# One token block's group norm moved into the recurrence's last four steps, and the output weights into memory that frees earlier

## The chip, the cores and the metric

One core of a Trainium2 chip runs the whole kernel. The metric is the device time of one execution in microseconds (us).

## What is computed

One layer of a backbone over 2048 latent tokens of width 1024, with 256 context tokens, all in float32. The parts that matter here, cut from the reference:

```
    h = modulate(rmsnorm(x, norm1_g), shift1, scale1)
...
    q, k, v, rw, gl = jnp.split(h @ w_in, IN_SPLITS, axis=-1)
...
    ya = latent_window_attention(q, k, v, kc, vc, sink)
...
    for d, rev in enumerate((False, True)):
...
        _, y_d = wkv7_scan(S_ctx, r_l, dec_l, kk_l, b_l, k_l, v_l, rev, True)
...
    yr = rwkv_output(y_lat[0] + y_lat[1], r_l, v_l, hg_l, dirs_l, gate_g2, r_k, lnx_w, lnx_b)
    x = x + gate1 * merge_branches(ya, yr, gl, w_branch_attn, w_branch_rwkv, w_out)
    x = x + gate2 * sq_relu_mlp(modulate(rmsnorm(x, norm2_g), shift2, scale2), w_mlp_up, w_mlp_down)

def rwkv_output(y, r, v, hg, dirs, gate_g2, r_k, lnx_w, lnx_b):
...
    mu = jnp.mean(y, axis=-1, keepdims=True)
    var = jnp.mean(jnp.square(y - mu), axis=-1, keepdims=True)
    yn = (y - mu) * lax.rsqrt(var + LNX_EPS)
...
    out = (yn.reshape(B, L, RWKV_WIDTH) * lnx_w + lnx_b + bonus.reshape(B, L, RWKV_WIDTH)).astype(hg.dtype)
    g = jax.nn.sigmoid(hg) @ gate_g2
    return out * g

def merge_branches(ya, yr, gate_logits, w_branch_attn, w_branch_rwkv, w_out):
    ga, gr = jnp.split(jax.nn.sigmoid(gate_logits), N_BRANCHES, axis=-1)
    return (ga * (ya @ w_branch_attn) + gr * (yr @ w_branch_rwkv)) @ w_out
```

Each float32 matmul runs as three: every operand is split in a high part (rounded by ScalarE) and a low part (the rest, by GpSimd or VectorE), and hi x hi, lo x hi and hi x lo are added up in PSUM.

## The kernel before

The program has four stages. The first makes projections and the recurrence's inputs. The second is the recurrence in 36 steps of 64 tokens per direction (`chain_g`, `chain_u`, `chain_s`, tiles `ch`, `gb`, `tb`), grouped in nine windows of four; while a window runs, the small triangular inverses of the next are made in the tiles `ga`, `st`, `au` and `itmp` of the pool `ip`, so that in the last window these lie idle. Tokens 512 to 1023 have their last contribution from either direction long before the last window. Each step has six parts; after each part `beside` adds a piece of the attention (`attend`, 16 blocks and a tail), and a piece of the filler (`fill`: gates, then `branch` for four blocks t = 0..3 of 512 tokens, the product of the attention's output with `w_branch_attn`, eight column tiles j of 12 matmuls each, tile `gt`, L988 to L990; VectorE scales each by its gate at L991 and the result is stored to `ma_d`). Block t = 3 can only begin when the last attention block is stored (`ya_d`). At the head of each step one piece of `ada2` is made as well (tile `adp`: four of the six modulation vectors, from 32 loads of 512 KB).

The third stage (merge, L1108 to L1263) goes over four blocks of 512 tokens in the order 1, 0, 2, 3. For a block, `rwkv_out` (L1139) does group norm, affine and gate, token tile by token tile, then splits the result in `yr_h` and `yr_l`. A loop over eight column tiles j multiplies by `w_branch_rwkv` (tile `mb`, L1240 to L1242, 96 matmuls a block), and VectorE adds the attention's part and the gate (tile `gt`, two buffers, L1243 and L1244) before the split to `m_h` and `m_l`. Then 192 matmuls a block multiply by `w_out` (tile `mm`, L1258 to L1260), and `second_norm` prepares the channel mixer's input in `h2_d`. In block 1 alone `merge_weights` (L1202) stands behind the j loop: it spreads gate1 and gate2 over the partitions (`dg` L1212), then for each of eight k loads 512 KB of `w_out` into the two-buffer tile `x1t` (L1220), multiplies it by gate1 on VectorE (L1223, two halves), and splits it in `wo_h` (ScalarE, L1224) and `wo_l` (GpSimd and VectorE by turns, L1225). The fourth stage is the channel mixer (L1265 to the end; up-projection tile `fu`, down-projection tile `fd`), whose first loads (`split_raw`, L1283) share two `raw` buffers.

The order on each engine is fixed before the run: a scheduler goes through the program with a time simulation, and what it decides stands in each engine's queue. SyncE (SP) alone issues all DMAs, in its own queue's order, so that a load that waits for a buffer holds up every DMA behind it. Pools are laid out in SBUF in the order in which they are opened; a tile that lies over memory of an earlier pool waits for the last user of that memory.

Of the kernel before, what the change touches and what calls it, by code (L numbers as in the profile page):

```python
# [7 lines left out]
F32 = mybir.dt.float32  # L8
# [8 lines left out]
P = 128  # L17
D = 1024
# [29 lines left out]
def tile_hybrid_block(ctx: ExitStack, tc: tile.TileContext, io: dict, out: bass.AP):  # L48
# [14 lines left out]
    ya_d = dram.tile([NP, P, SEQ], F32, name="ya_d")  # L63
    ma_d = dram.tile([KC, P, SEQ], F32, name="ma_d")
    bon_d = dram.tile([NP, P, SEQ], F32, name="bon_d")
    sg_d = dram.tile([96, SEQ], F32, name="sg_d")
# [487 lines left out]
    def bank(pl, name, tag):  # L554
        return pl.tile([P, 512], F32, name=name, tag=tag)
# [463 lines left out]
    def fill():  # L1019
# [17 lines left out]
        for t in range(SEQ // GBL):  # L1037
            while outs < (t + 1) * GBL // P:
                yield
            yield from branch(brp, raw_of, wa, t)  # L1040

    att, flr = attend(), fill()
    TICKS, EARLY = 1.0, 24
    credit = 0.0

    def beside(ticks):
# [6 lines left out]
        if credit >= 1:  # L1053
            next(att, None)
            credit -= 1

    mods = (x for m in range(4) for x in ada2(m))
    sts = []
# [16 lines left out]
    for w in range(NWIN):  # L1075
        ahead_of = window(w + 1, sts) if w + 1 < NWIN else iter(())
        for step in range(w * WS, w * WS + WS):
            nxts = [open_step(step + 1, d) if step + 1 < NCH else None for d in range(2)]
            for part in range(6):
                if part == 0:  # L1080
                    for s in cur:
                        chain_g(s)
                    next(mods, None)
                elif part == 1:
                    for s in cur:
                        chain_u(sts[w], s)
                elif part == 2:
                    chain_s(cur, nxts)
                elif part == 3 and nxts[0] is not None:
                    for s in nxts:  # L1090
                        turn(s)
                elif part > 3 and nxts[0] is not None:
                    before(nxts[part - 4])
                next(ahead_of, None)
                beside(TICKS)
            cur = nxts
        for _ in ahead_of:
            pass
    for _ in att:
        pass  # L1100
    for _ in flr:
        pass
    p2.close()
# [9 lines left out]
    gate2 = late.tile([P, D], F32, name="gate2")  # L1113
    p3 = ExitStack()
    mo = p3.enter_context(tc.tile_pool(name="mo", bufs=1, reuse_waits="tile"))
    mw = p3.enter_context(tc.tile_pool(name="mw", bufs=1, reuse_waits="tile"))
    mb = p3.enter_context(tc.tile_pool(name="mb", bufs=2, reuse_waits="tile"))
    mp = p3.enter_context(tc.tile_pool(name="mp", bufs=2, reuse_waits="tile"))
    mpb = p3.enter_context(tc.tile_pool(name="mpb", bufs=3, space=PSUM, reuse_waits="tile"))
# [19 lines left out]
    def rwkv_out(tb):  # L1139

        t0 = tb * TB
        yT = mp.tile([P, NP, TB], F32, name="yT", bufs=1)
        for i in range(TB // C):
# [54 lines left out]

    wo_h = mo.tile([P, KC, D], F32R, name="wo_h")
    wo_l = mo.tile([P, KC, D], F32R, name="wo_l")  # L1200

    def merge_weights():  # L1202
# [3 lines left out]
        gate1 = [mw.tile([P, 512], F32, name="gate1", tag="wt", bufs=2) for hf in range(2)]  # L1206
        for m, half, dst in ((0, 0.5, gate1), (3, 1.0, (gate2[:, 0:512], gate2[:, 512:D]))):
            for hf in range(2):
                ps = mtr.tile([P, 512], F32, name="mt")
                for k in range(4):  # L1210
                    dg = mw.tile([P, P], F32, name="dg", tag="x1t", bufs=2)
                    dve.tensor_scalar(out=dg, in0=ident, scalar1=mod2[:, m, hf * 4 + k:hf * 4 + k + 1],  # L1212
                                      scalar2=half, op0=ALU.mult, op1=ALU.mult)
                    pe.matmul(ps[:, k * P:(k + 1) * P], ones, dg, start=True, stop=True)
                dve.tensor_copy(dst[hf], ps)

        w_out = io["w_out"].rearrange("(k p) n -> p k n", p=P)
        for k in range(KC):
            raw = mw.tile([P, D], F32, name="x1t", bufs=2)
            sp.dma_start(out=raw, in_=w_out[:, k])  # L1220
            for hf in range(2):
                cs = slice(hf * 512, (hf + 1) * 512)
                dve.tensor_tensor(out=raw[:, cs], in0=raw[:, cs], in1=gate1[hf], op=ALU.mult)  # L1223
            act.activation(wo_h[:, k], raw, AF.Copy)  # L1224
            (pool, dve)[k % 2].tensor_tensor(out=wo_l[:, k], in0=raw, in1=wo_h[:, k].bitcast(F32), op=ALU.subtract)  # L1225

    blocks = (1, 0, 2, 3)
    br = rwkv_out(blocks[0])
    for at, tb in enumerate(blocks):
        t0 = tb * TB  # L1230
        mh = mo.tile([P, KC, TB], F32R, name="m_h", bufs=1)
        ml = mo.tile([P, KC, TB], F32R, name="m_l", bufs=1)
        for j in range(KC):
# [11 lines left out]
            split(mh[:, j], ml[:, j], gt[:, 0])  # L1245
        if at == 0:
            merge_weights()
        if at + 1 < len(blocks):
            br = rwkv_out(blocks[at + 1])
        for i in range(TB // P):  # L1250
            x = mw.tile([P, D], F32, name="x1t", bufs=2)
            sp.dma_start(out=x, in_=io["x"][t0 + i * P:t0 + (i + 1) * P])
            for hf in range(2):
                cs = slice(hf * 512, (hf + 1) * 512)
                ps = mps.tile([P, 512], F32, name="mm")
                for k in range(KC):
                    lh, ll = mh[:, k, i * P:(i + 1) * P], ml[:, k, i * P:(i + 1) * P]
                    pe.matmul(ps, lh, wo_h[:, k, cs], start=(k == 0), stop=False)  # L1258
                    pe.matmul(ps, lh, wo_l[:, k, cs], start=False, stop=False)  # L1259
                    pe.matmul(ps, ll, wo_h[:, k, cs], start=False, stop=(k == KC - 1))  # L1260
                dve.tensor_tensor(out=x[:, cs], in0=ps, in1=x[:, cs], op=ALU.add)
# [227 lines left out]
```

## Time and profile before

| | us |
|---|---|
| median of 3 runs | 4223.32 |
| lowest, highest | 4220.43, 4228.75 |
| the profiled execution | 4228.56 |
| its span in the trace | 4226.8 |
| PE busy | 3865.3 (91%) |
| DVE busy | 2171.9 (51%) |
| ACT busy | 1359.5 (32%) |
| POOL busy | 1349.6 (32%) |
| mean granted clock of TensorE | 0.932 |

PE is TensorE (PEld its weight loads), DVE VectorE, ACT ScalarE, POOL GpSimd, SP SyncE (SPq, PEq: what their sequencers do). A share of busy time is a mean over stages; what a stage is worth is read from that stretch of the trace. Times within the span are given from its start.

### The profile page before, as it was taken

Reading aid. Unit: us, or ns where it says so; the run is one execution under the profiler, and the core shown is the slowest. Engines: PE = TensorE matmul, PEld = TensorE weight load, DVE = VectorE, ACT = ScalarE, POOL = GpSimd, SP = SyncE. Lnnn points to the kernel's source line nnn. Section 1 sums busy time; section 2 is a strip of 40 time slices with the busy share of each in tenths; the row PEclk is TensorE's granted clock in tenths of the full one; section 3 lists DMA queues with packets and bytes.
Section 4 is the critical chain, followed back from the end, with each engine's and each line's share of the span. In section 5 each row is a group of like instructions: output and inputs, shape, how many; then the busy total and the mean of one; then the engine's idle time right before and its main releaser. Section 6 shows DMA issues by size and latency. Waiting matters only on the chain.

```text
span 4226.8 us, 67796 instructions
## 1 busy us (share of the span) xinstructions
PE 3865.3 (91%) x26788; PEld 3148.4 (74%) x26788; DVE 2171.9 (51%) x3794; ACT 1359.5 (32%) x2476; POOL 1349.6 (32%) x1104
## 2 busy tenths in 40 slices
PE   7989978897899989888898779989999999999999
PEld 5778868785677767766676658768888888888887
DVE  3355277767576366556566364444443345444334
ACT  2353444554343333322322233331212213112121
POOL 3353555554221110000000174533433334443231
PEclk8999979897999989797897889999999999999999
DMA  6665566666544445343442545542211214211111
GB/s 236 202 195 158 161 183 188 188 185 184 164 138 138 125 131 148 106 132 96 131 139 83 158 150 179 176 154 65 70 50 40 60 41 130 69 60 60 40 55 45
DMA packets 617587, 529.95 MB, mean 125 GB/s; under 512 B 156212, under 2 KB 536340, under 8 KB 616244
## 3 DMA queue, kind: packets, MB, share of 16 engines
q1 hardware_dynamic: 617268, 525.60, 41.6%
q8 instruction: 211, 3.46, 0.3%
q14 instruction: 108, 0.88, 0.1%
HBM read 381.09 MB, written 144.38 MB: 124 GB/s over the span
## 4 chain that ended last, share of the span: by engine, by line
PE 58%; DVE 6%; DMA 4%; issue 2%; POOL 2%; SPq 1%; ACT 1%; POOLq 0%; DVEq 0%; ACTq 0%
PE fd L1343 5%; PE fd L1344 5%; PE fd L1345 5%; PE fu L235 5%; PE fu L236 5%; PE fu L237 5%; PE ch L535 5%; PE gt L947 3%; PE ops L883 3%; PE gb L535 2%; DVE au L582 1%; PE sc L835 1%; PE mm L1260 1%; PE mm L1258 1%; PE mm L1259 1%
## 5 line engine op out<-in xcount | busy, mean ns | idle before, releaser
L235 PE MATMUL acc<-hh,w_hi 128*128 128x384 f32 (+6 forms) x1304 | 457.4, 353 | 41.6 <-ACT hh L211 18.9
L237 PE MATMUL acc<-hh,w_lo 128*128 128x384 f32 (+6 forms) x1304 | 455.8, 351 | 10.3 <-POOL w_lo L229 10.3
L236 PE MATMUL acc<-hl,w_hi 128*128 128x384 f32 (+6 forms) x1304 | 456.5, 351 | 4.8 <-POOL hl L212 4.8
L1349 DVE TENSOR_TENSOR acc<-fd,acc 128x512 f32<-128x512 f32 x480 | 322.3, 686 | 249.1 <-PE fd L1345 246.8
L235 PE MATMUL fu<-h2h,up_h 128*128 128x512 f32 x1024 | 403.4, 394 | 5.8 <-ACT rl L1330 5.8
L1343 PE MATMUL fd<-dn_h,g_h 128*128 128x512 f32 x1024 | 399.8, 390 | 3.5 <-DVE acc L1347 3.5
L236 PE MATMUL fu<-h2l,up_h 128*128 128x512 f32 x1024 | 402.6, 393 | 0.0
L237 PE MATMUL fu<-h2h,up_l 128*128 128x512 f32 x1024 | 402.0, 393 | 0.0
L1333 DVE TENSOR_TENSOR g_l<-rl,g_h 128x512 fp32r<-128x512 f32 x128 | 150.0, 1173 | 487.4 <-POOL rl L1332 487.4
L1344 PE MATMUL fd<-dn_l,g_h 128*128 128x512 f32 x1024 | 399.7, 390 | 0.0
L1345 PE MATMUL fd<-dn_h,g_l 128*128 128x512 f32 x1024 | 398.3, 390 | 0.0
L235 PEld LDWEIGHTS acc<-hh,w_hi 128*128 128x128 f32 (+2 forms) x1304 | 256.1, 197 | 67.1 <-ACT hh L211 21.8
L1332 POOL TENSOR_TENSOR rl<-rl 128x512 f32<-128x512 f32 x128 | 149.9, 1171 | 469.2 <-ACT g_h L1331 469.1
L229 POOL TENSOR_TENSOR w_lo<-w_raw,w_hi 128x1024 fp32r<-128x1024 f32 (+1 forms) x92 | 232.7, 2532 | 205.9 <-ACT w_hi L228 185.7
L1330 ACT ACTIVATE rl<-fu 128x512 f32<-128x512 f32 x128 | 76.2, 597 | 654.1 <-PE fu L237 644.9
L237 PEld LDWEIGHTS acc<-hh,w_lo 128*128 128x128 f32 (+2 forms) x1304 | 255.7, 196 | 31.4 <-POOL w_lo L229 12.5
L236 PEld LDWEIGHTS acc<-hl,w_hi 128*128 128x128 f32 (+2 forms) x1304 | 256.0, 196 | 25.1 <-POOL hl L212 6.0
L1287 POOL TENSOR_TENSOR dn_l<-raw,dn_h 128x1024 fp32r<-128x1024 f32 x64 | 155.6, 2450 | 275.1 <-ACT dn_h L1286 275.1
L845 DVE TENSOR_REDUCE mm<-sc 128x1 f32<-128x256 f32 (+1 forms) x256 | 119.0, 477 | 237.9 <-PE sc L837 152.2
L235 PEld LDWEIGHTS fu<-h2h,up_h 128*128 128x128 f32 x1024 | 193.1, 189 | 49.3 <-ACT rl L1330 6.0
L1343 PEld LDWEIGHTS fd<-dn_h,g_h 128*128 128x128 f32 x1024 | 192.9, 188 | 44.9 <-DVE acc L1347 4.0
L237 PEld LDWEIGHTS fu<-h2h,up_l 128*128 128x128 f32 x1024 | 192.7, 188 | 43.5
(305 smaller groups left out, 8292.3 us busy)
## 6 DMA issues: line engine op xcount, KB each, us to landing
w_raw<-in_w_in SPq DMA_DIRECT2D x74, 512.0 KB
raw<-in_w_mlp_up SPq DMA_DIRECT2D x64, 512.0 KB
raw<-in_w_mlp_down SPq DMA_DIRECT2D x64, 512.0 KB
bk_d<-bk SPq DMA_DIRECT2D x36, 512.0 KB
w<-v_d SPq DMA_DIRECT2D x144, 128.0 KB
gw_raw<-in_w_in SPq DMA_DIRECT2D x32, 512.0 KB
ada_w<-in_w_ada SPq DMA_DIRECT2D x32, 512.0 KB
gt<-g_d SPq DMA_DIRECT2D x64, 256.0 KB
```

Of the source, the lines that this page charges most:

```text
L229: pool.tensor_tensor(out=lo[:, :, :m], in0=raw[:, :, :m], in1=hi[:, :, :m].bitcast(F32), op=ALU.subtract)
L235: pe.matmul(ps[:m, :n], wh[:, k, :m], hh[:, k, :], start=(k == 0), stop=False)
L236: pe.matmul(ps[:m, :n], wh[:, k, :m], hl[:, k, :], start=False, stop=False)
L237: pe.matmul(ps[:m, :n], wl[:, k, :m], hh[:, k, :], start=False, stop=(k == KC - 1))
L535: return self.link(nc.tensor.matmul(*a, **k))
L1287: eng.tensor_tensor(out=lo, in0=raw, in1=hi.bitcast(F32), op=ALU.subtract)
L1332: pool.tensor_tensor(out=rl, in0=rl, in1=rl, op=ALU.mult)
L1333: dve.tensor_tensor(out=glo[:, j], in0=rl, in1=gh[:, j].bitcast(F32), op=ALU.subtract)
L1343: pe.matmul(ps, lh, dn[j][0][:, cs], start=(j == 0), stop=False)
L1344: pe.matmul(ps, lh, dn[j][1][:, cs], start=False, stop=False)
L1345: pe.matmul(ps, ll, dn[j][0][:, cs], start=False, stop=(j == FG - 1))
L1349: dve.tensor_tensor(out=acc[:, cs], in0=ps, in1=acc[:, cs], op=ALU.add)
```

## The change

A new generator `early` does the group norm, affine, bonus and gate of block 1 (tokens 512 to 1023) in the last window, steps 32 to 35, in four pieces of 128 tokens, nine calls a step; it works in the inverse's idle tiles and in PSUM that the attention uses, and stores its result to `yw_d`. `rwkv_out` of block 1 is left with four loads and the split. The pieces of `ada2` come at one and two a step by turns, so that they end with step 23 and not with step 35. `merge_weights` is emitted ahead of block 1's j loop, and the spreading of gate2 behind its loop over k. The tiles `wo_h` and `wo_l` are cut into one per k; k = 0..3 lie in a new pool `mv` and k = 4..7 in `mo`, and the pool `mp` comes first, which moves every pool behind it in SBUF: `mv` now lies at the memory that the attention had, k = 4..7 over the attention branch's weights, and the channel mixer's pool `fw` (its first `up_h`, `up_l` and half of `h2`) comes to lie over `mv`. The core of the diff:

```diff
+    EB0, EBN = 512, 512
+    yw_d = dram.tile([NP, P, EBN], F32, name="yw_d")
...
+    def early():
+        wk = [ip.tile([P, 4, NP, P], F32, name="yw0", tag="ga", bufs=1), ip.tile([P, 4, NP, P], F32, name="yw1", tag="st")]
+        aw = ip.tile([P, 1024], F32, name="g2e", tag="au", bufs=1)
+        sg = ip.tile([P, 2, P], F32, name="sge", tag="itmp", bufs=1)
+        g2 = aw[0:96, 0:512]
+        sp.dma_start(out=g2, in_=io["gate_g2"])
...
+        for i in range(EBN // P):
+            yT, yc, yw, bt = (wk[i % 2][:, j] for j in range(4))
...
+            ps = bank(atp, "ey", "at")
+            for p in range(NP):
+                pe.transpose(ps[:, p * P:(p + 1) * P], yT[:, p], ident)
+            y3 = ps.rearrange("p (h c) -> p h c", c=C)
+            dve.tensor_reduce(out=s1[:, 0], in_=y3, axis=AX.X, op=ALU.add)
+            dve.tensor_scalar(out=s1[:, 0], in0=s1[:, 0], scalar1=-1.0 / C, scalar2=None, op0=ALU.mult)
...
+            dve.tensor_tensor(out=y3c, in0=y3, in1=s1[:, 0].unsqueeze(2).broadcast_to([P, H, C]), op=ALU.add)
+            act.activation(yw, yc, AF.Square)
+            dve.tensor_reduce(out=s1[:, 1], in_=yw.rearrange("p a b -> p (a b)").rearrange("p (h c) -> p h c", c=C),
+                              axis=AX.X, op=ALU.add)
+            pool.tensor_scalar(out=s1[:, 1], in0=s1[:, 1], scalar1=1.0 / C, scalar2=1e-5 * C, op0=ALU.mult, op1=ALU.add)
+            pool.tensor_tensor(out=s1[:, 1], in0=s1[:, 1], in1=expo[:, :H], op=ALU.pow)
+            pool.tensor_tensor(out=y3c, in0=y3c, in1=s1[:, 1].unsqueeze(2).broadcast_to([P, H, C]), op=ALU.mult)
+            yield
+            ps = bank(atp, "eb", "at")
+            for p in range(NP):
+                pe.transpose(ps[:, p * P:(p + 1) * P], yc[:, p], ident)
+            for p in range(NP):
+                act.activation(yw[:, p], ps[:, p * P:(p + 1) * P], AF.Identity, scale=col(O_LW + p), bias=col(O_LB + p))
+            pool.tensor_tensor(out=yw, in0=yw, in1=bt, op=ALU.add)
+            yield
+            gp = bank(atp, "eg", "at")
+            for p in range(NP):
+                pe.matmul(gp[:, p * P:(p + 1) * P], g2[:, p * P:(p + 1) * P], sg[0:96, i % 2], start=True, stop=True)
+            dve.tensor_tensor(out=yw, in0=gp.rearrange("p (a t) -> p a t", a=NP), in1=yw, op=ALU.mult)
+            sp.dma_start(out=yw_d[:, :, i * P:(i + 1) * P].rearrange("a p t -> p a t"), in_=yw)
+            yield
+
...
                 if part == 0:
                     for s in cur:
                         chain_g(s)
-                    next(mods, None)
+                    for _ in range(1 + step % 2):
+                        next(mods, None)
...
+                if w == NWIN - 1:
+                    ey = ey or early()
+                    for _ in range(2 - part % 2):
+                        next(ey, None)
                 beside(TICKS)
...
-    for _ in att:
-        pass
-    for _ in flr:
-        pass
+    for it in (ey, att, flr):
+        for _ in it:
+            pass
...
+    mp = p3.enter_context(tc.tile_pool(name="mp", bufs=2, reuse_waits="tile"))
     mo = p3.enter_context(tc.tile_pool(name="mo", bufs=1, reuse_waits="tile"))
     mw = p3.enter_context(tc.tile_pool(name="mw", bufs=1, reuse_waits="tile"))
     mb = p3.enter_context(tc.tile_pool(name="mb", bufs=2, reuse_waits="tile"))
-    mp = p3.enter_context(tc.tile_pool(name="mp", bufs=2, reuse_waits="tile"))
+    mv = p3.enter_context(tc.tile_pool(name="mv", bufs=1, reuse_waits="tile"))
...
         t0 = tb * TB
+        if EB0 <= t0 < EB0 + EBN:
+            yh = mp.tile([P, NP, TB], F32R, name="yr_h", bufs=1)
+            yl = mp.tile([P, NP, TB], F32R, name="yr_l", bufs=1)
+            for p in range(NP):
+                yw = mp.tile([P, TB], F32, name="yw")
+                sp.dma_start(out=yw, in_=yw_d[p, :, t0 - EB0:t0 - EB0 + TB])
+                split(yh[:, p], yl[:, p], yw)
+            return yh, yl
...
-    wo_h = mo.tile([P, KC, D], F32R, name="wo_h")
-    wo_l = mo.tile([P, KC, D], F32R, name="wo_l")
+
+    wo_h = [(mv if k < KC // 2 else mo).tile([P, D], F32R, name=f"wo_h{k}") for k in range(KC)]
+    wo_l = [(mv if k < KC // 2 else mo).tile([P, D], F32R, name=f"wo_l{k}") for k in range(KC)]
...
-        for m, half, dst in ((0, 0.5, gate1), (3, 1.0, (gate2[:, 0:512], gate2[:, 512:D]))):
+        def along(m, half, dst):
...
 
+        along(0, 0.5, gate1)
         w_out = io["w_out"].rearrange("(k p) n -> p k n", p=P)
         for k in range(KC):
...
-            act.activation(wo_h[:, k], raw, AF.Copy)
-            (pool, dve)[k % 2].tensor_tensor(out=wo_l[:, k], in0=raw, in1=wo_h[:, k].bitcast(F32), op=ALU.subtract)
+            act.activation(wo_h[k], raw, AF.Copy)
+            (pool, dve)[k % 2].tensor_tensor(out=wo_l[k], in0=raw, in1=wo_h[k].bitcast(F32), op=ALU.subtract)
+        along(3, 1.0, (gate2[:, 0:512], gate2[:, 512:D]))
...
     blocks = (1, 0, 2, 3)
     br = rwkv_out(blocks[0])
+    merge_weights()
     for at, tb in enumerate(blocks):
...
             split(mh[:, j], ml[:, j], gt[:, 0])
-        if at == 0:
-            merge_weights()
         if at + 1 < len(blocks):
             br = rwkv_out(blocks[at + 1])
```

**TensorE at the recurrence's end.** Before, the last products of the recurrence (`ch`) are followed by the attention branch of block t = 3 (`gt`), and this by the group norm's transposes (`yT`, `yc`) and the gate's products (`sgt`), ahead of the first `mb`; a piece of that:

```order
L990 MATMUL gt<-ya_h,wa_l 128x512
L1149 MATMUL mt<-ident,yT 128x128 x12
L1170 MATMUL mt<-ident,yc 128x128 x2
L1177 MATMUL mt<-sgt,g_24326 128x512
L1170 MATMUL mt<-ident,yc 128x128 x6
L1177 MATMUL mt<-sgt,g_24326 128x512
L1170 MATMUL mt<-ident,yc 128x128 x4
L1240 MATMUL mb<-yr_h,br_hi 128x512 x2
```

With the change, the same place reads:

```order
L991 MATMUL gt<-ya_h,wa_h 128x512
L992 MATMUL gt<-ya_l,wa_h 128x512
L993 MATMUL gt<-ya_h,wa_l 128x512
L1313 MATMUL mb<-yr_h,br_hi 128x512
L1314 MATMUL mb<-yr_l,br_hi 128x512
L1315 MATMUL mb<-yr_h,br_lo 128x512
```

The `mb` products follow straight on the branch. Of the branch's 96 matmuls 6 stand ahead of the recurrence's last one with the change, and 60 before it; the other 90 and 36 come behind it.

**VectorE at the same place**, from the recurrence's last addition (`ysb`) on. Before:

```order
L734 TENSOR_TENSOR ysb<-ch_24122,yo 128x256
L991 SCALAR_TENSOR_TENSOR gt<-gt 128x512 x2
L1152 TENSOR_REDUCE s_24344<-mt 128x8
L1153 TENSOR_SCALAR s_24344<-s_24344 128x8
L1155 TENSOR_TENSOR yc<-mt,s_24344 128x512
L1158 TENSOR_REDUCE s_24344<-ysq 128x8
L991 SCALAR_TENSOR_TENSOR gt<-gt 128x512
```

With the change (L994 is the old L991, L1294 the old L1223, L1296 the old L1225):

```order
L737 TENSOR_TENSOR ysb<-ch_24269,yo 128x256
L1294 TENSOR_TENSOR x1t<-x1t,gate_24509 128x512
L1294 TENSOR_TENSOR x1t<-x1t,gate_24510 128x512
L994 SCALAR_TENSOR_TENSOR gt<-gt 128x512 x2
L1296 TENSOR_TENSOR wo_l_24482<-x1t,wo_h_24474 128x1024
L1294 TENSOR_TENSOR x1t<-x1t,gate_24509 128x512
L1294 TENSOR_TENSOR x1t<-x1t,gate_24510 128x512
L994 SCALAR_TENSOR_TENSOR gt<-gt 128x512
```

The making of the output weights now stands between the gates of the attention branch, where the group norm stood.

**SyncE at the start of the channel mixer.** Before, the first loads for it stand ahead of the loads of the last block's third and fourth token tile (`x1t<-in_x`):

```order
L1283 DMA raw<-in_w_mlp_up 128x8x128 x2
L1262 DMA x_d<-x1t 128x1024
L1283 DMA raw<-h_d 128x1024 x4
L1283 DMA raw<-in_w_mlp_up 128x8x128
L1262 DMA x_d<-x1t 128x1024
L1283 DMA raw<-in_w_mlp_up 128x8x128
L1197 DMA h_d<-h2f 128x512
L1283 DMA raw<-h_d 128x1024
L1252 DMA x1t<-in_x 128x1024
```

With the change:

```order
L1323 DMA x1t<-in_x 128x1024
L1354 DMA raw<-in_w_mlp_up 128x8x128 x2
L1266 DMA h_d<-h2f 128x512
L1431 DMA gfb<-in_gf 128x1024
L1333 DMA x_d<-x1t 128x1024
L1354 DMA raw<-h_d 128x1024
L1266 DMA h_d<-h2f 128x512
L1354 DMA raw<-h_d 128x1024
```

They now come after the last token tile's load, and the `h2` loads (`raw<-h_d`) after its store. On TensorE the first `fu` stood 22 matmuls of its kind ahead of the last `mm` before, and stands 16 transposes behind it now.

## Rows read from the trace of the kernel before

**Rows 1.** The page, part 1: busy time, share of the span, instructions of each engine.

```profile
PE 3865.3 (91%) x26788; PEld 3148.4 (74%) x26788; DVE 2171.9 (51%) x3794; ACT 1359.5 (32%) x2476; POOL 1349.6 (32%) x1104
```

**Rows 2.** Busy us by stretch: PE, PEld, DVE, ACT, POOL, PEclk, DMA share, GB/s.

```profile
2400.00:2440.00 40.00, 22.83 (x101) 15.17 (x97) 13.87 (x26) 6.53 (x11) 18.23 (x19) 0.74 0.56 159
2440.00:2480.00 40.00, 32.80 (x151) 24.00 (x150) 28.31 (x43) 12.95 (x21) 29.98 (x23) 0.96 0.51 158
2480.00:2520.00 40.00, 29.86 (x84) 18.11 (x85) 31.44 (x34) 14.48 (x18) 32.10 (x21) 0.65 0.57 169
2520.00:2560.00 40.00, 39.99 (x188) 32.58 (x188) 18.05 (x33) 10.71 (x21) 14.92 (x19) 1.00 0.38 130
```

**Rows 3.** PE's timeline at the recurrence's end: start, us, what, idle before.

```profile
2399.68 1.15 PE L535 MATMUL ch<-kr,w 64*64 64x64 f32 x32
```

**Rows 4.** Chain of waits, 2385 to 2450: start us, us, what.

```profile
2390.85 3.47 DMA ma_d<-gt
...
2439.05 0.70 PE mb L1240 x2
```

**Rows 5.** Chain of waits, 2450 to 2560.

```profile
2456.62 4.46 DMA gt<-g_d
...
2462.69 0.64 ACT m_h L1128
2463.40 1.31 POOL m_l L1129
...
2498.20 3.70 DMA x1t<-in_w_out
2501.99 3.47 DVE x1t L1223 x2
...
2506.59 0.79 PE mm L1258
...
2558.51 0.23 PE mm L1260
```

**Rows 6.** VectorE by line, 2400 to 2512: xcount, busy us, mean ns, idle before.

```profile
L1223 DVE TENSOR_TENSOR x1t<-x1t,gate 128x512 f32<-128x512 f32 x14 | 17.7, 1302 | 2.0 <-DMA x1t<-in_w_out 2.0
...
L1155 DVE TENSOR_TENSOR yc<-mt,s 128x512 f32<-128x512 f32 x8 | 5.5, 685 | 0.2
...
L1225 DVE TENSOR_TENSOR wo_l<-x1t,wo_h 128x1024 fp32r<-128x1024 f32 x3 | 3.7, 1221 | 1.1 <-ACT wo_h L1224 1.1
```

**Rows 7.** GpSimd by line, the same stretch.

```profile
L1160 POOL TENSOR_TENSOR s<-s,expo 128x8 f32<-128x8 f32 x8 | 13.1, 1640 | 0.6
...
L1225 POOL TENSOR_TENSOR wo_l<-x1t,wo_h 128x1024 fp32r<-128x1024 f32 x3 | 7.5, 2509 | 0.0
```

**Rows 8.** TensorE's waits, 2340 to 2425: us in total, times, longest.

```profile
PE gt L988 <- ACT ya_h L978: 4.4, 1, 4.4
```

**Rows 9.** Tile adp over the span: duration min/median/max, first and last start.

```profile
L117 PE MATMUL adp<-ada_w,silr x256: 376/403/637, 1126.7 to 2369.2; 128*32 128x256 f32 x128
```

**Rows 10.** Chain of waits, 2770 to 2860.

```profile
2774.65 0.46 PE fu L235 x2
...
2797.30 0.24 PE mm L1260
...
2799.91 3.72 DMA raw<-h_d
2803.65 1.07 ACT h2h L1286
2804.74 1.24 DVE h2l L1287
...
2823.00 2.73 POOL up_l L1287
```

**Rows 11.** TensorE's waits, 2795 to 2850.

```profile
PE fu L235 <- ACT rl L1330: 5.8, 1, 5.8
PE fd L1343 <- DVE acc L1347: 3.5, 1, 3.5
```

More of the change, by code (lines that the diff above doesn't have):

```diff
@@ L1040, in fill, with load @@
             yield from branch(brp, raw_of, wa, t)
+    def early():
[4 more added lines that the diff above has]
+        sp.dma_start(out=g2, in_=io["gate_g2"])
+        def load(i):
+            t0 = EB0 + i * P
+            for j in range(P // C):
+                sp.dma_start(out=wk[i % 2][:, 0, :, j * C:(j + 1) * C], in_=y_d[t0 // C + j])
+            sp.dma_start(out=sg[0:96, i % 2], in_=sg_d[:, t0:t0 + P])
+            sp.dma_start(out=wk[i % 2][:, 3], in_=bon_d[:, :, t0:t0 + P].rearrange("a p t -> p a t"))
+        load(0)
+        for i in range(EBN // P):
+            yT, yc, yw, bt = (wk[i % 2][:, j] for j in range(4))
+            s1 = aw[:, 512 + i % 2 * 2 * H:512 + (i % 2 + 1) * 2 * H].rearrange("p (b h) -> p b h", h=H)
+            if i + 1 < EBN // P:
+                load(i + 1)
+            ps = bank(atp, "ey", "at")
[4 more added lines that the diff above has]
+            dve.tensor_scalar(out=s1[:, 0], in0=s1[:, 0], scalar1=-1.0 / C, scalar2=None, op0=ALU.mult)
+            ycf = yc.rearrange("p a b -> p (a b)")
+            y3c = ycf.rearrange("p (h c) -> p h c", c=C)
+            dve.tensor_tensor(out=y3c, in0=y3, in1=s1[:, 0].unsqueeze(2).broadcast_to([P, H, C]), op=ALU.add)
[19 more added lines that the diff above has]
+            yield
@@ L1055, in beside @@
             credit -= 1
+    ey = None
     mods = (x for m in range(4) for x in ada2(m))
@@ L1257, in tile_hybrid_block @@
                     lh, ll = mh[:, k, i * P:(i + 1) * P], ml[:, k, i * P:(i + 1) * P]
-                    pe.matmul(ps, lh, wo_h[:, k, cs], start=(k == 0), stop=False)
-                    pe.matmul(ps, lh, wo_l[:, k, cs], start=False, stop=False)
-                    pe.matmul(ps, ll, wo_h[:, k, cs], start=False, stop=(k == KC - 1))
+                    pe.matmul(ps, lh, wo_h[k][:, cs], start=(k == 0), stop=False)
+                    pe.matmul(ps, lh, wo_l[k][:, cs], start=False, stop=False)
+                    pe.matmul(ps, ll, wo_h[k][:, cs], start=False, stop=(k == KC - 1))
                 dve.tensor_tensor(out=x[:, cs], in0=ps, in1=x[:, cs], op=ALU.add)
```

## The prediction, made before the change ran

> **What bounds the kernel now.** I read the page first: TensorE is busy for 91% of the span and VectorE, next to it, for 51% [rows 1]. Over the whole kernel, then, time is gained where TensorE idles or runs slowly. The busy times by stretch show where: between 2400 and 2520 TensorE is busy for 22.8, 32.8 and 29.9 of each 40 us, at a granted clock of 0.74, 0.96 and 0.65, and from 2520 on for all of 40 at 1.00 [rows 2]. The reader is to see a hole of 120 us right behind the recurrence, with full work on either side. Its edges come from two more views. The last product of the recurrence starts at 2399.68 and lasts 1.15, so the recurrence ends at T0 = 2400.8 [rows 3]; the last `mm` of block 1 ends at 2558.7 [rows 5]. The stretch thus takes 157.9 us. In it stand 36 `gt`, 117 `mb` (96 of block 1, the others of block 0) and 192 `mm` matmuls: 345 at 0.23 us each, as a matmul at full clock follows the other [rows 5], are 79.4 us, and the transposes are small. So some 70 us are idle or half speed.
>
> The chain of waits says what fills them. The first `mb` comes only at 2439.05 [rows 4], because the group norm lies ahead of it: on GpSimd alone each token tile takes 1.64 us for one operation (L1160) [rows 7], and every transpose behind it waits. Then the `mb` are paced by their gates, each a load of 4.46 us, VectorE, 0.64 on ScalarE and 1.31 on GpSimd before a buffer is free [rows 5]. Last come the output weights: a load of 3.70 at 2498.2, two multiplications of 3.47 together, and only at 2506.6 the first `mm` [rows 5]. Three chains follow one another. The change takes the first out, and puts the third beside what is left.
>
> **The change, part by part.** The sum is made on the profiled execution (4228.56, span 4226.8); it was 5.2 us above the median of 4223.32, and I apply the differences to the median. A difference of 0.2%, 8.4 us, is what a measurement of this kernel can tell from none.
>
> *Stretch from T0 to block 1's last `mm`.* The order on TensorE puts 90 `gt`, 96 `mb` and 192 `mm` here now: 378 x 0.23 = 87 us, so what can be won at most is 157.9 - 87 = 71, less the transposes. I do not expect that, since three waits remain.
> 1. The attention branch. `gt` has two buffers, so two columns cost one chain of store (3.47 [rows 4]), load of the next gates (priced as 4.46 [rows 5]), one VectorE operation (0.69, the like-shaped L1155 [rows 6]) and some 0.7 of issuing: 9.3 us. Eight columns are 37 us. The first column's 12 matmuls at half clock are 12 x 0.46 = 5.5, and two halves of `x1t` ahead of a gate on VectorE cost 2 x 1.30 [rows 6] = 2.6. Together 45 us.
> 2. The `mb` products. Two columns are ready when the branch ends. The weights k = 4..7 lie over the branch's weights and so wait for its end; SP's queue has the loads of later columns behind the last `x1t`, which need a `wo_h` (about 1.1) and a `wo_l` on GpSimd (2.5 [rows 7]) and a load (3.7 [rows 5]): 8 us. Then three pairs of 4.46 + 0.64 + 1.31 + 0.69 + 1.2 for VectorE's second operation and the issue = 8.3, or 25. First pair 6, and four halves of `x1t` on VectorE 5. Together 44.
> 3. The 192 `mm` are 44 us at full clock; a part of the first tile fits in the gaps of 2, against that stand its last wait and `second_norm`'s transposes. I take 44.
>
> The sum is 133, against 157.9: **-25**. If VectorE's halves and the SP queue cost nothing and the chains overlap, 1 and 2 are 33 and 40 and the `mm` 40: 113, or -45. If every `x1t` multiplication takes 1.74 (the 3.47 of two [rows 5]) and falls in the path with four `wo_l` of 1.22 [rows 6], 16 x 1.74 + 4 x 1.22 = 32.7 where 8 are counted: 158, or 0.
>
> On VectorE and GpSimd the row shows the same L1223 at a mean of 1.30 us, against 0.69 for L1155 of the same size with one operand in PSUM [rows 6]; beside it GpSimd ran `wo_l` of 2.51 [rows 7]. The Trainium skill, SBUF — State Buffer, section "SBUF: two separate sides", says that a VectorE operation with both inputs in SBUF and a GpSimd operation that reads SBUF take one port pair by a lock, and the later blocks for the whole of the other. That agrees with the row; by it alone the group norm's removal from GpSimd would bring the 16 halves towards 0.69 each, some 10 us less on VectorE, and the stretch to about 123 instead of 133. I keep 1.30, since GpSimd still makes four `wo_l` and the low parts of `m` there.
>
> *Block 0.* It has 13 more of its own `mb` behind the point measured: 13 x 0.23 = **+3**.
>
> *The last four steps.* TensorE loses 54 `gt` (54 x 0.23 = 12.4) and the `adp` pieces, and gets 48 transposes and small matmuls of the group norm and some `dg`: about 7 us less work. VectorE gets for each of four pieces four operations of about 0.69 [rows 6] and a small one, 12 us in all; it is an engine on which the recurrence waits, in queue order, though half idle. GpSimd gets four of its 1.64 and three shorter ones each, and is idle in these steps otherwise. The wait for the last attention block's store and reload (4.4 us [rows 8]) stays, and now falls in the last step. I take **-3**, between -11 (all work saved) and +9 (all of VectorE's 12 on the path, less part of TensorE's).
>
> *`ada2`.* 256 small matmuls over the recurrence [rows 9], none added or removed; twice as dense up to step 23. Its pieces and its 32 loads are moved past the attention's query loads, with which it shares one buffer; **-1**, between -6 and +6, as nothing in the trace ranks it.
>
> *Start of the channel mixer.* Before, 22 of the first `fu` stood ahead of the last `mm` (the first at 2774.65, the last `mm` at 2797.30 [rows 10]), and two waits remained, 5.8 and 3.5 us [rows 11]. With the change the first `up` weights lie over `mv`, which is read until the last `mm`. Behind it come `up_h` (1.07), `up_l` for two tiles on GpSimd (2.73 each [rows 10]), and with two `raw` buffers two rounds of `h2`: 3.72 + 1.07 + 1.24 = 6.0 each [rows 10]. 1.1 + 2.7 + 2.7 + 2 x 6.0 = 18.5, less the 16 transposes that still run: about 17 us of idle TensorE. Against 9.3 before that is **+8**; it is 0 if the raw loads come early enough to take a round off and the later waits go, +17 if both waits of before stay behind it.
>
> The sum: -25 + 3 - 3 - 1 + 8 = **-18**, or 4223.3 - 18 = 4205 us.
>
> **The rivals.**
> *A. The hole closes.* The branch, now dense behind T0, covers the weights' making wholly, and the stretch takes 113 us: -45 + 3 - 3 + 5 = -40, 4183 us. For it: VectorE is busy for only 28 to 31 of 40 us even where it hurts [rows 2]. Against it: two gate buffers and one SP queue pace both loops.
> *B. Nothing is gained.* The weights' chain was last before and is last again: VectorE makes it between branch and `mb`, both of which wait behind it in its queue, and the stretch takes some 150 us. -8 + 3 + 8 = +3 with nothing at the steps: 4226, within 8 either way. For it: multiplications of 1.74 at 2502 [rows 5].
> *C. Slower, by the channel mixer's start.* `mv` under `fw` makes TensorE wait a full chain: 18.5 us to the first `fu`, then two more rounds of `h2` (12) and an `up_l` (2.7) with 12 us of `fu` work to hide them, the next down weights behind them on GpSimd: 25 us more than before. It decides against the change once the stretch gains less than that: at 142 us (-16), with +3 and +25, it is +12, 4235 us. For it: VectorE and GpSimd split those weights, and the clock falls after a long idle, as the 0.65 of 2480 to 2520 shows [rows 2]. Against it: the up weights' raw loads are free of `mv` and can come early.
>
> **How the numbers follow.** My forecast has 0.56, A 0.13, B 0.18, C 0.13. The forecast's own range, by its bounds, is 4187 to 4219; of its chance 0.52 lies beyond 8.4 us below. With A that is faster 0.65; same is B nearly whole and a rest of the forecast, 0.20; slower is C and a rest of B, 0.15. The range from 4182 to 4230 leaves out half of A and most of C, 2 in 10.
>
> **What would show it.** In the changed profile I look for the group norm's lines (`ey`, `eb`, `eg`) between the last four steps with T0 within 10 us of 2400, whatever the rest shifts; `mb` starting about 45 us behind T0 and closing at about 90; the last `mm` of block 1 at T0 + 133; idle of about 17 us ahead of the first `fu`. The forecast is wrong if the first `mm` again follows a `wo_h` chain with TensorE idle for over 10 us at one go (B), if the last `mm` comes before T0 + 118 (A), or if the idle between the last `mm` and steady `fd` exceeds 30 us (C). If T0 moves by more than 10 us, the steps' term was mis-sized.

## The result, and the profile after

The changed kernel took 4190.53 us (median of 5 runs, 4189.42 to 4198.52) against 4223.32 (5 runs, 4220.43 to 4228.75): a ratio of 0.9919, 95% interval 0.9906 to 0.9933, 33 us faster. The forecast was 4205 (18 faster) within 4182 to 4230. The profiled execution took 4198.52, with a span of 4196.7; it is the slowest of its five, as the one of before was among the slower of its own. The two traces differ by 30 us.

Where those 30 us are is read from five edges. First TensorE's timeline at the recurrence's end, in the changed kernel (start us, us, what), which answers to [rows 3]:

```profile
2369.17 1.15 PE L538 MATMUL ch<-kr,w 64*64 64x64 f32 x32
```

Then SyncE's timeline: the last store of `x_d` of each of the four blocks of the merge, of before

```profile
2559.50 0.32 SPq L1262 DMA_DIRECT2D x_d<-x1t  x1
...
2637.07 0.32 SPq L1262 DMA_DIRECT2D x_d<-x1t  x1
...
2716.47 0.32 SPq L1262 DMA_DIRECT2D x_d<-x1t  x1
...
2798.28 0.32 SPq L1262 DMA_DIRECT2D x_d<-x1t  x1
```

and of the changed kernel:

```profile
2511.19 0.32 SPq L1333 DMA_DIRECT2D x_d<-x1t  x1
...
2599.55 0.32 SPq L1333 DMA_DIRECT2D x_d<-x1t  x1
...
2682.70 0.32 SPq L1333 DMA_DIRECT2D x_d<-x1t  x1
...
2759.86 0.33 SPq L1333 DMA_DIRECT2D x_d<-x1t  x1
```

The time from each edge to the next is the length of a stage:

| stage (us) | before | after | difference | forecast |
|---|---|---|---|---|
| to T0, the recurrence's end | 2400.8 | 2370.3 | -30.5 | -4 |
| T0 to block 1's last store | 158.7 | 140.9 | -17.8 | -25 |
| block 0 | 77.6 | 88.4 | +10.8 | +3 |
| block 2 | 79.4 | 83.2 | +3.8 | 0 |
| block 3 | 81.8 | 77.2 | -4.6 | 0 |
| channel mixer to the end | 1428.5 | 1436.8 | +8.3 | +8 |

So the stages behind T0 together give nothing in this pair of traces, and the whole difference lies ahead of T0. That edge scatters: four traces of kernels with the changed kernel's order up to T0 have it at 2370.3, 2374.8, 2383.3 and 2390.2, a spread of 20 us, so that much can be chance between two traces. ScalarE's timeline places it. The first copy `g<-ch` of step 32, before and after:

```profile
2319.31 0.38 ACT L687 ACTIVATE g<-ch 128x256 f32<-128x256 f32 x1 [3.67 <-PE ch L535]
```

```profile
2292.84 0.39 ACT L690 ACTIVATE g<-ch 128x256 f32<-128x256 f32 x1 [4.21 <-PE ch L538]
```

26.5 of the 30.5 us are there ahead of step 32, before `early` has computed anything; the last four steps, where it works, give only 4.0. Not all of the 26.5 need be the change's. In a later trace of the changed kernel with ada2 put back, whose order up to there is that of before but for `early`'s first loads, the copy stands 15.6 us ahead of before's:

```profile
2303.76 0.39 ACT L690 ACTIVATE g<-ch 128x256 f32<-128x256 f32 x1 [3.67 <-PE ch L538]
```

The hole behind T0 is smaller, not closed: the busy time by stretch of the changed kernel (columns as in [rows 2], which it answers, about 30 us earlier).

```profile
2360.00:2400.00 40.00, 27.49 (x178) 19.00 (x178) 14.70 (x24) 11.01 (x19) 16.21 (x12) 0.79 0.87 262
2400.00:2440.00 40.00, 31.75 (x112) 23.48 (x111) 22.65 (x22) 9.09 (x12) 16.87 (x10) 0.85 0.43 142
2440.00:2480.00 40.00, 35.72 (x159) 28.59 (x158) 23.66 (x42) 9.84 (x17) 23.85 (x24) 0.89 0.57 172
2480.00:2520.00 40.00, 40.00 (x190) 31.52 (x189) 17.12 (x28) 15.13 (x27) 18.16 (x19) 1.00 0.50 167
```

TensorE's waits from 2380 to 2560 name what is left, as [rows 8] did (us in total, times, longest):

```profile
PE gt L991 <- DVE gt L994: 12.7, 6, 4.2
PE mm L1329 <- ACT m_h L1189: 3.6, 2, 2.5
PE mm L1329 <- DVE x1t L1332: 3.2, 1, 3.2
```

and the chain of waits there (start us, us, what) shows its members, as [rows 4] and [rows 5] did:

```profile
2398.60 4.54 DMA ma_d<-gt
...
2404.47 5.96 DMA ma_d<-gt
...
2411.82 0.79 PE gt L991
...
2421.10 0.23 PE mb L1313
...
2459.93 5.59 DMA x1t<-in_x
...
2466.36 0.80 PE mm L1329
2467.16 0.43 PE mm L1330
```

Block 1's group norm and the wait for `wo_h` are gone. The branch, now dense behind T0, waits for its own gates, whose stores take 4.5 to 6.0 us where one of before took 3.47.

### The profile page after: what moved, and what is told of

Its sections match the earlier page's. It is cut to its first block, busy times and chain, and to the rows that moved or that the text cites. A ratio compares the mean times of both kernels' runs of the same rounds, so it can differ in the third digit from the quotient of the medians.

```text
span 4196.7 us, 67793 instructions
## 1 busy us (share of the span) xinstructions
PE 3850.3 (92%) x26753; PEld 3147.2 (75%) x26812; DVE 2172.7 (52%) x3794; ACT 1361.4 (32%) x2488; POOL 1339.1 (32%) x1104
## 5 line engine op out<-in xcount | busy, mean ns | idle before, releaser
L238 PE MATMUL acc<-hh,w_hi 128*128 128x384 f32 (+6 forms) x1304 | 458.5, 354 | 37.3 <-ACT hh L214 16.9
L1404 DVE TENSOR_TENSOR g_l<-rl,g_h 128x512 fp32r<-128x512 f32 x128 | 158.8, 1241 | 476.5 <-POOL rl L1403 476.5
L239 PEld LDWEIGHTS fu<-h2l,up_h 128*128 128x128 f32 x1024 | 193.0, 188 | 43.5 <-DVE h2l L1358 0.8
```

The lines of the kernel that those rows point to most:

```text
L238: pe.matmul(ps[:m, :n], wh[:, k, :m], hh[:, k, :], start=(k == 0), stop=False)
L239: pe.matmul(ps[:m, :n], wh[:, k, :m], hl[:, k, :], start=False, stop=False)
L1404: dve.tensor_tensor(out=glo[:, j], in0=rl, in1=gh[:, j].bitcast(F32), op=ALU.subtract)
```

## The experiments

Ratios are medians of runs against the kernel before on the same chip, with 95% intervals. Single executions of one kernel lie up to 20 us either side of the median in these batches, so stages are read from traces, and sums from the ratios.

### The three parts alone

```diff
-                    next(mods, None)
+                    for _ in range(1 + step % 2):
+                        next(mods, None)
```

> The kernel before with one edit: ada2's pieces come one and two a step by turns. In the changed kernel the recurrence's end came 30 us earlier than before (2370 against 2401 in the two profiled executions), most of it between steps 21 and 33. Theory 'ada2' (its pieces gone from steps 24 to 35 give the gain): the recurrence ends 20 to 30 us earlier here too, the rest stays as before, and the time is 20 to 30 us below before. Rival 'early' (the branch products pushed out of the last steps give it): the recurrence ends within 5 us of before, the time within 6. Rival 'chance of the schedule' (any edit shuffles the order and moves the end by 10 us or so, either way): the end moves, but by steps other than 21 to 33.

4206.99 against 4222.52, ratio 0.9955 (0.9939 to 0.9972): by the ratio 19 us from this line alone, just short of the 20 expected at least. T0 stands at 2389.0, 11.8 us earlier than before and not 20 to 30, and step 32 at 2297.1. The theory's words are not met either: steps 21 to 23, in which pieces still come, gain as well.

```diff
+    def early():
...
+                    for _ in range(2 - part % 2):
+                        next(ey, None)
...
+        if EB0 <= t0 < EB0 + EBN:
```

> The kernel before with early() and the shortened rwkv_out of block 1 alone; ada2, the order of merge_weights and the pools as before. Theory 'ada2': the recurrence's end stays within 10 us of before. The group norm is gone from behind it, but the output weights' chain still comes last and paces the first mm, so of the stretch from the recurrence's end to block 1's last mm (158 us) some 10 to 15 are gained; time 8 to 16 us below before. Rival 'early': the end comes 20 us or more earlier and the time falls by 30. Rival 'the weights' chain hides it all': the stretch stays within 5 us of 158 and the time within 5 of before.

4234.93, ratio 1.0030 (1.0013 to 1.0048): slower by 0.3%. The last four steps are 8.6 us shorter, but the stretch behind T0 grows from 158.7 to 169.9. Busy time by stretch shows a hole that is later and deeper than that of [rows 2]:

```profile
2480.00:2520.00 40.00, 22.36 (x68) 14.01 (x66) 31.37 (x36) 13.22 (x16) 27.92 (x18) 0.73 0.52 151
```

and the chain of waits says that in it the output weights' loads and multiplications follow each other:

```profile
2477.13 3.78 DMA x1t<-in_w_out
2480.94 2.35 DVE x1t L1289 x2
...
2484.49 3.37 DVE x1t L1289 x2
2487.88 1.07 ACT wo_h L1290
2488.97 1.23 DVE wo_l L1291
...
2490.49 4.74 DMA x1t<-in_w_out
```

From 2501.7 to 2522.4 the chain then goes through block 0's group norm on GpSimd, beside the last two `wo_l`. No theory had it slower: all 96 matmuls of the branch now stand behind T0, where 36 stood, and the weights' chain, now with block 0's group norm, is still last.

```diff
+    merge_weights()
     for at, tb in enumerate(blocks):
...
-        if at == 0:
-            merge_weights()
```

(with the tiles per k and the pools' order of the changed kernel)

> The kernel before with merge_weights ahead of block 1's loop, its tiles per k in the new places, and the pools' new order; no early(), ada2 as before. Theory (the weights' chain and the group norm follow each other, and taking either out leaves the other): the stretch of 158 us loses 10 to 20, block 0 loses some of it again, and the channel mixer's start costs 8 us as it did in the changed kernel; time within 8 us of before. Rival (the weights were the whole wait): the stretch loses 30 or more and the time falls by 15 or more.

4227.45, ratio 1.0013 (0.9992 to 1.0033): no gain, as the theory had it. The stretch falls to 143.9, 14.8 less; block 0 takes 87.4 (+9.8) and the mixer 1435.9 (+7.4). Block 0's rise is in part work that before was done while TensorE waited for the weights: 21 of its `mb` matmuls stood ahead of block 1's last `mm` before and none does now, 4.8 us at 0.23 each. In part it is waiting: TensorE waits 6.0 us there for `m_h`, `m_l` and a gate, where before it waited 0.9.

### Pairs, and the changed kernel again

```diff
-                    for _ in range(1 + step % 2):
-                        next(mods, None)
+                    next(mods, None)
```

(on the changed kernel)

> The changed kernel with ada2 put back to one piece a step: early() and the move of merge_weights together. Alone, ada2's move gave a ratio of 0.9955, early() 1.003 and the move of merge_weights 1.0013; all three give 0.9919. Theory (early and merge_weights only pay together: each takes out one of two chains that end at about the same time): ratio to before 0.995 to 0.998, that is 8 to 20 us, and the stretch from the recurrence's end to block 1's last mm at 135 to 145 us. Rival (ada2's end is what makes the rest pay): ratio 1.002 or more.

```diff
-                if w == NWIN - 1:
-                    ey = ey or early()
...
-        if EB0 <= t0 < EB0 + EBN:
```

(on the changed kernel)

> The changed kernel without early(), block 1's group norm behind the recurrence as before: ada2 and merge_weights moved. If the parts add up, 0.9955 x 1.0013 = 0.997, 13 us below before. Theory (early pays with merge_weights ahead): 0.995 to 0.998, and the stretch at 140 to 150 us with the group norm's transposes in it; early is then worth some 15 us in the changed kernel. Rival (early is worth nothing, or costs, in the changed kernel too): 0.990 to 0.993, as fast as the changed kernel or faster.

> The changed kernel once more, beside the others on one chip: single executions differ by up to 15 us either way here, so the parts are to be compared on the same chip. Expected 0.992 (within 0.0015). In its profile the recurrence's end should again come 10 to 30 us earlier than 2401; if it stands near 2390, as in the run with the mixer's pools, then half of the 30 us of the first profile was the scatter of one execution.

| ada2 moved | early | merge_weights moved | ratio (95%) | us of 4222 |
|---|---|---|---|---|
| yes | | | 0.9955 (0.9939 to 0.9972) | -19 |
| | yes | | 1.0030 (1.0013 to 1.0048) | +13 |
| | | yes | 1.0013 (0.9992 to 1.0033) | +5 |
| | yes | yes | 0.9969 (0.9955 to 0.9984) | -13 |
| yes | | yes | 0.9972 (0.9958 to 0.9985) | -12 |
| yes | yes | yes | 0.9934 (0.9919 to 0.9949) | -28 |

The changed kernel again comes out as expected. `early` alone costs 13 us, and with `merge_weights` ahead it gives 16 to 19: the theory that the two pay only together holds, with stretches of 142.0 (`early` and `merge_weights`) and 142.8 (ada2 and `merge_weights`) as expected. ada2's move gives 15 to 19 in the three companies tried. So the work on the hole is worth 13 us together (7 to 19 by its interval), and the move of ada2, one line of the diff, as much or more.

### What ada2's move takes away

```diff
-            wt = ap_.tile([P, D], F32, name="ada_w2", tag="qraw", bufs=1)
-            sp.dma_start(out=wt, in_=w_ada[:, k, (2 + m) * D:(3 + m) * D])
+            wt = vtok.rearrange("p a b c -> p (a b c)")[:, 0:D]
```

> The kernel before with ada2's 32 loads left out: its matmuls stand where they were, one piece a step, but read a tile that is in memory already (the modulation vectors are not the reference's), so that nothing shares the buffer of the attention's query loads. Theory 'loads' (the wait for the shared buffer and the 512 KB loads slow the attention in the late steps): 12 to 30 us below before, as the move of ada2 (19 us) or more. Rival 'matmuls' (the pieces' work on TensorE in steps that it fills is the cost): within 5 us of before.

4169.38 against 4221.65, ratio 0.9869 (0.9845 to 0.9892): by the ratio 55 us faster, with every matmul of ada2 in its place, and far beyond the 30 that the theory had. The matmuls are not the cost.

```diff
-                    next(mods, None)
+                    if step < 24:
+                        next(mods, None)
```

> The kernel before with ada2's pieces simply left out from step 24 on (the last 12 of 36 are not made; the modulation vectors that they give are constants), and one a step as before up to step 23. It has what the move of ada2 takes from the late steps without what it adds to the early ones. If the early steps hide the added pieces, it equals the move: 17 to 21 us below before. If they cost there (the starts of steps 18 to 20 came 7 to 12 us later in two of the profiles with the move), it is 24 to 32 below. Rival 'it is the order that the schedule happens to take, not the pieces': within 8 us of before.

4216.81, ratio 0.9989 (0.9973 to 1.0005): 5 us by the medians. My theory for the single part ("its pieces gone from the late steps give the gain") falls with this: without any piece from step 24 on, the time is within 8 us of before, as the rival said, and step 32 starts at 2312.0, where the move of the pieces had 2297.1. That rival, the order that the schedule happens to take, is thus not excluded for the move.

Between the two results stands the buffer. Before, ada2's weights (`ada_w2`) lie in the one buffer of the attention's query loads (`qraw`). A query load waits until the last piece's matmuls have read the weights, the next weights wait until the query is split, and all of them stand in SP's one queue.

```diff
-            wt = ap_.tile([P, D], F32, name="ada_w2", tag="qraw", bufs=1)
+            wt = ap_.tile([P, D], F32, name="ada_w2", bufs=1)
...
-        ob = gap.tile([P, GBL], F32, name="gob", bufs=2)
+        ob = gap.tile([P, GBL], F32, name="gob", tag="graw", bufs=2)
```

> The kernel before with one edit of memory: ada2's weights get a buffer of their own instead of sharing the attention's query buffer (the 4 KB come from the gates' output tile, which now shares the two small load buffers of the filler's first part). Loads, matmuls and their steps stay, one piece a step. Without the loads the kernel took 54 us less; leaving out the last 12 pieces gave 5 only. Theory 'shared buffer' (query load, then weights, then query load wait for one another in SP's queue, and the attention and everything behind it in that queue with them): most of the 54 comes, 30 to 55 us below before, the recurrence's end near 2350 to 2370. Rival 'the loads' traffic and their places in SP's queue': within 12 us of before.

4171.31 against 4225.73, ratio 0.9867 (0.9847 to 0.9888): by medians 54 us, with all loads made. So their traffic is not the cost. Their places in the queues did not stay, though: with the new buffer the scheduler takes another order, on ScalarE from 1193 us on. What the 54 us owe to waits that are gone and what to this order is not separated; both come from the buffer. T0 stands at 2349.7, and every other stage is within 3 us of before. Nearly all of the gain is there at step 24 already, 48.1 us of it. ScalarE's first copy `g<-ch` of that step, before and with the buffer of its own:

```profile
2034.63 0.39 ACT L687 ACTIVATE g<-ch 128x256 f32<-128x256 f32 x1 [1.14 <-PE ch L535]
```

```profile
1986.54 0.38 ACT L687 ACTIVATE g<-ch 128x256 f32<-128x256 f32 x1 [1.50 <-PE ch L535]
```

Leaving out the pieces from step 24 on could thus give little: most of the cost lies ahead of them. The view of the tile `qraw` shows the wait itself (us, times until each releaser; then who waited for it). Before:

```profile
  ACT qA L812: 33.9, 12
  DMA qraw<-q_d: 23.9, 10
  PE sT L873: 3.4, 3
who waited for it (us, times):
  DVE qA L815: 33.9, 12
  ACT qB L814: 23.9, 10
  PE sc L835: 11.9, 3
```

After the change:

```profile
  ACT qA L815: 36.5, 7
  DMA qraw<-q_d: 16.9, 10
  PE sT L876: 0.9, 1
who waited for it (us, times):
  DVE qA L818: 36.5, 7
  ACT qB L817: 16.9, 10
  PE sc L838: 6.4, 3
```

With a buffer of its own:

```profile
  ACT qA L812: 12.6, 7
  PE sT L873: 11.6, 8
  DMA qraw<-q_d: 1.1, 1
who waited for it (us, times):
  DVE qA L815: 12.6, 7
  ACT qB L814: 1.1, 1
```

ScalarE waits 23.9 us for query loads before, 16.9 after, 1.1 with the own buffer; TensorE's scores (`sc`) wait 11.9, 6.4 and not at all. The order of the times is the order of these waits. ScalarE's waits group the same way in all the other traces: 22.5 to 26.4 us in the four without ada2's move, 17.3 to 18.8 in the five with it, and 1.1 in the two without the loads or with the buffer of its own. The 54 us are more than the waits' sum. Behind a waiting ScalarE stand the recurrence's own copies in the same queue, and TensorE's mean granted clock over the whole span rises from 0.932 in the trace of before to 0.943 in this one; how the 54 divide between the two I have not separated. The run without the last 12 pieces fits this: it gave little, and ScalarE still waits 22.5 us in it. By what way the move of the pieces shortens the wait is not settled: it changes which loads meet in the buffer up to step 23, and in the part alone steps 20 to 23 shrink with it.

### The start of the channel mixer, and all together

```diff
+    fa = p4.enter_context(tc.tile_pool(name="fa", bufs=1, reuse_waits="tile"))
     hp = p4.enter_context(tc.tile_pool(name="h2", bufs=1, reuse_waits="tile"))
...
-        raw = fw.tile(list(hi.shape), F32, name="raw", bufs=2)
+        raw = fa.tile(list(hi.shape), F32, name="raw", bufs=2)
```

(and with it, in `fa`, the first two pairs of up weights and the high half of the first `h2`)

> The changed kernel with one more edit: the channel mixer's first tiles (raw buffers, the up weights of the first two column tiles, the high half of h2) lie in a pool of their own where the merge's pool mp lay, and the low half of h2 at the end of memory, so that none of them lies over the output weights in mv. In the changed kernel TensorE idled between 2760 and 2782 and the part from the last store of the merge to the end took 1436.8 us, against 1428.5 before. Theory (the place over mv costs those 8 us): that part comes back to 1428 to 1431, and the time is 5 to 9 us below the changed kernel's 4190. Rival (the order of the two raw buffers costs it, wherever they lie): 1435 or more, time within 3 us of the changed kernel.

> The changed kernel with the mixer's first tiles in a pool of their own, once more, beside the changed kernel on one chip. Its profile had 1423.9 us from the merge's last store to the end, against 1436.8 in the changed kernel, yet its median over 4 runs was no lower. Theory (the 13 us are real and were hidden by scatter): median 8 to 13 us below the changed kernel of the same batch, ratio to before near 0.989. Rival (given back elsewhere): within 4 us of the changed kernel.

Ratios of 0.9919 (0.9894 to 0.9945) and 0.9925 (0.9907 to 0.9943); medians of 4191.95 and, beside the changed kernel's 4193.13, 4190.00. The stage itself fell in both traces, from 1436.8 and 1436.3 to 1423.9 and 1424.3, further than the 1428 to 1431 expected. TensorE's waits from 2755 to 2830 in the changed kernel, which answer to [rows 11],

```profile
PE mt L1259 <- ACT h2f L1263: 11.5, 2, 5.8
PE fu L238 <- ACT h2h L1357: 3.1, 1, 3.1
PE mt L1259 <- DVE x1t L1254: 2.7, 1, 2.7
```

are together 17.3 us, the size of the hole that the forecast put there. Most of it stands at the transposes of `second_norm` (`mt`), though, with no `fu` ready to fill it, and not at the first `fu`. With the mixer's first tiles moved, little more than this is left of it from 2755 to 2850 in the first of the two traces:

```profile
PE mt L1259 <- ACT h2f L1263: 4.7, 2, 4.4
```

So the place in memory is its cause. That the whole time falls with it is not shown: the median is 3.1 us below the changed kernel's, within the 4 us of the rival, and the intervals overlap. In the two traces of that batch T0 came 8.5 us later with the edit, at an order that is the same up to there.

> The changed kernel with the mixer's pools apart (as in the run before of that kind, ratio 0.9925), ada2 at one piece a step again, and ada2's weights in a buffer of their own. If the shared buffer is the cause, the move of ada2 (17 us) is replaced by the whole of its cost (30 to 55): 4150 to 4175, ratio 0.983 to 0.989, faster than the changed kernel. If the traffic is the cause: 4200 to 4210, slower than the changed kernel by the 17 us that the move gave.

4139.19 against 4225.73, ratio 0.9794 (0.9772 to 0.9815), below the 4150 expected at least and faster than both kernels: 87 us under before and, by the ratios, some 50 to 60 under the changed one, though not measured beside it. T0 stands at 2328.8, the stretch takes 141.5 and the mixer 1425.3.

## Why the prediction was right, and where it was not

*The sign and the range* were right; the time came out 14 us below the forecast, and only in part for the reasons that I gave. The parts other than ada2 were forecast at -17 together; `early` and `merge_weights` without ada2's move measured -13 (-19 to -7), so there the account held in size. At least as much again came from ada2, which the sum had at -1. That the time stayed in the range with that term some 10 us outside its own bounds is luck.

*The step that failed* is the one on ada2: "-1, between -6 and +6, as nothing in the trace ranks it". It measured -15 to -19. I named the shared buffer in that very step and priced it at nothing. The trace of before did show a wait there, though not its price of 54 us: the view of the tile `qraw`, shown above, has TensorE waiting 11.9 us in 3 waits for a query and ScalarE 23.9 in 10. I had asked for `adp`, which showed only matmuls [rows 9], and not for the tile that lay in the same place. My sign for T0, within 10 us of 2400, failed in the first pair (30.5), but it would have blamed the last four steps, and the cause was this term, together with the scatter of that edge.

*The hole.* -25 was forecast for the stretch, of 133 us. It took 140.9 and in the next three traces of the same order 133.2, 135.2 and 134.7: 136.0 on the mean, -22.7. The parts: the branch was to end at T0 + 45 and `mb` to begin there; the first `mb` came at 2421.1, T0 + 50.8, with gates' stores of up to 6.0 where I had 3.47. `mb` was to close at T0 + 89; its last product of block 1 ends at 2455.4, T0 + 85.1, so the loop took 34 where I had 44. The `mm` were to take 44 behind that; they ended 55 later, at T0 + 140.1, although 28 of the 192 had started within the loop. The other 164 took 44, the first of them at 0.43 each (until 2472) where one at full clock takes 0.23; the waits for `x1t` and `m_h` were 4.3 and the transposes and small products between them 7. So errors of +6, -10 and +11 stand in the parts. Rival A, that the hole closes, did not come about: `gt` still waits 12.7 us for its gates.

*Block 0* was mis-sized: +3 for 13 matmuls, +8 to +11 in every kernel with the weights moved. The count was wrong: of the 117 `mb` that I counted in the stretch 21 were block 0's, and in the changed kernel's trace none of them comes ahead of block 1's last `mm`, which makes +4.8. And what stood beside the weights' wait before was not only those products but, as far as the waits tell, the gates and splits that go with them: TensorE now waits for `m_h` and `m_l`, 4.7 us in block 0 of the trace, where before it waited 0.9. With `early` alone block 0 rose by 5.7 as well, so the move of the weights need not be all of it.

*The last four steps*: -3 was forecast; -4.0 was measured in the first pair, -2.8, -3.3 and +1.3 in the three further traces. But these hold two effects. With ada2 as before `early` shortens these steps from 81.5 to 72.9 and 72.6 us; with ada2 moved they take 91.9 and 88.1 without `early` and 77.5 to 82.8 with it. `early` is worth about 9 there, and ada2's move gives back some of what it gained ahead of them.

*The mixer's start*: +8 was forecast and +8.3 and +7.8 measured. It is rival C's mechanism at the forecast's price; C itself did not come about, as the stretch kept more than 16 us.

*Rival B* came true for the parts in its time, and only for `early` alone in its reason, the weights' chain that is last again. With `merge_weights` alone the stretch did fall, by 14.8, and block 0 and the mixer gave 17.2 back.

*The port rule.* L1223 fell from a mean of 1.30 us [rows 6] to 0.905 with block 1's group norm gone from GpSimd's queue there. This is VectorE's line in the changed kernel from 2370 to 2511:

```profile
L1294 DVE TENSOR_TENSOR x1t<-x1t,gate 128x512 f32<-128x512 f32 x16 | 13.8, 905 | 13.4 <-DMA x1t<-in_w_out 13.4
```

In the two kernels that have the weights moved but block 1's group norm still behind the recurrence, the same line took 1.52 and 1.56; in five with both moved, 0.94 to 0.95. It went the way of the rule in the Trainium skill, SBUF — State Buffer, section "SBUF: two separate sides": 6 of the 10 us that the rule gave came. But the line then waited 13.4 us for its loads, and how much of the 6 us reached the stretch is not shown.

## What to carry to other kernels

Before costing an edit that moves a step's loads, ask the trace for every tile that shares a buffer with the moved one, and who waits there; a tag with one buffer and two users is a queue, and its price does not stand in the rows of either user's matmuls. When two chains end at about the same time, taking out one may give nothing, and here it did or cost: test the parts alone and in pairs before crediting them. A tile moved in memory can have its bill at the next stage that lies over it; here the chain of loads and splits gave that bill to within 1 us.

## What was not expected

Executions of one kernel scatter by up to 20 us either way here: before ran from 4206.98 to 4237.12 in one batch of 23 and from 4206.63 to 4242.31 in one of 17, and T0 moves by 20 us at an unchanged order. The stage lengths behind T0 were steadier: the mixer's stage kept within 0.5 us between repeats (1436.8 and 1436.3, 1423.9 and 1424.3). One buffer shared by 16 query loads and 32 loads of weights carried 54 us of 4226.
